# Splitting the query and key weights one unit ahead, and a split with the token tile as outer loop

## The chip, the cores and the metric

The kernel runs on one core of a Trainium2 chip. Its time is the device time of one execution in microseconds (us); a run's figure is the time of that core. The engines are TensorE (PE, with its weight loads listed as PEld), VectorE (DVE), ScalarE (ACT), GpSimd (POOL) and SyncE (SP, which here only starts transfers). Each works through its own queue in order.

## What is computed

One layer of a decoder for 256 tokens of width 2048, with 256 memory tokens, all in float32. After a norm, one wide projection feeds four branches; gates weigh them, and an output projection closes the layer. Cut to what matters here:

```python
h = rms_norm(x, g_pre[l])
proj = h @ w_in[l]
(a_val, a_gate, sq, sk, sv, s_gate, cq, ck, cv, c_gate, c_lr,
 mq, m_gate, g_logits) = jnp.split(proj, split_at, axis=-1)
...
y_c = gla_mixer(cq, ck, cv, c_lr, c_gate, w_alpha[l], b_alpha[l], g_gla[l])
y_m = mem_attn(mq, m_gate, mem, g_mem[l], w_mem_kv[l])
gates = jax.nn.sigmoid(g_logits.reshape(B, S, N_BRANCH, D_MODEL) + b_merge[l])
merged = (gates[:, :, 0] * (y_a @ w_br_pool[l]) + gates[:, :, 1] * (y_b @ w_br_swa[l])
          + gates[:, :, 2] * (y_c @ w_br_gla[l]) + gates[:, :, 3] * (y_m @ w_br_mem[l]))
x = x + rms_norm(merged @ w_out[l], g_post[l])
```

The change touches the projections `cq` and `ck` (queries and keys of the gated linear attention), the key and value projections of the memory tokens ahead of them, and every block that is computed by `a_block`, among them the output projection `merged @ w_out`.

## The kernel before

**Split numbers.** Every float32 operand of a large matmul is split into a high part in the reduced type fp32r and a low part, the remainder. `split_w` does this for a piece of 1024 weight columns: ACT copies the raw weights to the high part (a tile named ...h), DVE subtracts it from the raw weights (a tile named ...l). A product is then three matmuls, high by high, high by low and low by high. The parts live in rings of five tiles each (`NB_HILO`), so a split waits until PE has read the split five before it. The raw weights come by transfers of up to 1 MB, started by SP, into a ring of thirteen buffers that the activations and other large tiles share.

**Two forms of a block.** `b_unit` computes 128 output columns for all 256 tokens: it loads the weights, splits them in two halves (`cq0` has `cq00` and `cq01`), and runs 16 pairs of matmuls, one with the high part against both parts of the activations (512 wide) and one with the low part (256 wide). Then `evac` reads the accumulator out, for `cq` and `ck` by `two_sums`: one copy on ACT and one addition on DVE. `b_split` does the split alone, so that it can stand earlier in the program; before, that is done for the unit `cq0` only. `a_block` computes up to 512 output columns with the tokens on the partitions, in two accumulators (`t` = 0, 1), one for each 128 tokens. It goes through the weights split by split, in each split over the pieces `kk`, in each piece over `t`, with the three matmuls of `mm3` innermost. It returns a function that reads out both accumulators; the caller calls it at once.

**Background work.** `queue` holds generators: the memory keys' read-out (`km_evac`: four evacuations of `km_acc`, then a norm), and `quarter_prep`, which builds sums and differences of quarters of the activations (DVE subtracts to `qs`, ACT and DVE split that to `quarter`). `pull(n)` runs n steps of the first one, at fixed points of the blocks; `drain` runs one to its end. From the third `ck` unit on `gates` does the same for the gate projections, whose weights are named gu, gt and gv.

**What sets the order.** The program is written as one stream; a scheduler then gives each engine its own order and places the waits. `tc.issue_after(i)` makes what is traced inside it stand behind instruction `i` on the engine of `i`. Before, it is used for the memory keys' evacuation (behind the split of `cq0`) and for the scaling of the memory values (behind the latest split).

**The stages that the prediction speaks of.** First the memory tokens' values and keys (`vma`, `kma`) with the norm of x and its four pieces `xhl` (line 309 forms the normed piece, 225 and 226 split it), then `cq0` to `cq3` and `ck0` to `ck3` (lines 191 and 192 are the two matmuls of a pair, 139 and 140 the split, 203 to 207 the evacuation), then the blocks `cv` with the first gates between them, and so on; the output blocks `o0` to `o3` come near the end (145 to 147 are the matmuls of `mm3`, 947 and 948 read an output block out).

Of the kernel before, what the change touches and what calls it, by code (L numbers as in the profile page):

```python
# [14 lines left out]
P = 128  # L15
# [5 lines left out]
SCALE = DH ** -0.5  # L21
# [16 lines left out]
def kernel(ctx, tc, ins, out):  # L38
# [34 lines left out]
    queue = []  # L73

    def pull(n):
        while n > 0 and queue:
            try:
                next(queue[0][1])
                n -= 1
            except StopIteration:  # L80
                queue.pop(0)

# [41 lines left out]

    last_split = [None, None]

    def new_raw():
# [20 lines left out]

    def a_block(name, units, stat, nw, evac, load=None, per_split=None, other=False):

        accs = [seven(f"{name}a{t}") if other else acc(f"{name}a{t}", [P, 512]) for t in range(2)]
        nk = 4 * len(units)
        for u, src in enumerate(units):
            raw = load_raw(src, 4 * nw) if load is None else load(u, src)
            nk_s = max(1, 1024 // nw) if per_split is None else per_split(u)
            for hf in range(4 // nk_s):
                hi, lo = split_w(raw[:, hf * nk_s * nw : (hf + 1) * nk_s * nw], nk_s * nw, f"{name}{u}{hf}")
                for kk in range(nk_s):
                    k = 4 * u + nk_s * hf + kk
                    ws = slice(kk * nw, (kk + 1) * nw)  # L160
                    for t in range(2):
                        sh, sl = stat(k)
                        ts = slice(t * P, (t + 1) * P)
                        mm3(accs[t][:, :nw], sh[:, ts], sl[:, ts], hi[:, ws], lo[:, ws], k == 0, k == nk - 1)
                if hf % 2 == 0:
                    pull(1)
                gates(nk_s * 6 * (nw / 2.4 + 14) * 1e-3)
            pull(1)
# [11 lines left out]
    def b_unit(name, src, mov, evac, ready=None):  # L180
# [4 lines left out]
        for hf in range(2):  # L185
            hi, lo = ready[hf] if ready else split_w(raw[:, hf * 1024 : (hf + 1) * 1024], 1024, f"{name}{hf}")
            for kk in range(8):
                k = 8 * hf + kk
# [4 lines left out]
            if hf == 0:  # L193
                pull(1)
                gates(2.8)
        evac(name, a)
        pull(1)
# [79 lines left out]
    def m_norm():  # L277
        yield from inv_rms_row("m", mcol)
        yield
        km, vm = kv["k"], kv["v"]  # L280
        with tc.issue_after(last_split[0]):
            for t in range(2):
                act.activation(vm[:, t, :], vm[:, t, :], AF.Copy, scale=mcol[:, t : t + 1])
# [30 lines left out]
    vm_acc = [acc(f"vma{t}", [P, 512]) for t in range(2)]  # L314
    km_acc = [seven(f"kma{h}") for h in range(4)]

    def mem_chunk(c):
# [37 lines left out]
        for j in range(2):  # L355
            hi, lo = split_w(rk[:, 1024 * j : 1024 * j + 1024], 1024, f"km{c}{j}")
            for i in range(2):
                a = km_acc[2 * j + i]
# [11 lines left out]
    def km_evac():  # L370
        km = kv["k"] = c4("km", [P, 4, T])
        for h in range(4):
            with tc.issue_after(cq0_split[0]), tc.issue_after(cq0_split[1]):
                two_sums(f"km{h}", km_acc[h], km[:, h, :])
            yield
# [3 lines left out]
    drain("xprep")  # L379
    cq0 = b_split("cq0", ins["w_cqk"][0])  # L380
    cq0_split = tuple(last_split)

# [283 lines left out]

    for h in range(4):
        b_unit(f"cq{h}", ins["w_cqk"][h], h_at, plain_evac(gq[:, h, :], SCALE), cq0 if h == 0 else None)
    for h in range(4):
        if h == 2:  # L670
            drain("quarters")
            gate_stream[0] = all_gates()
        b_unit(f"ck{h}", ins["w_cqk"][4 + h], h_at, plain_evac(gk[:, h, :]))
    for j in range(3):
# [277 lines left out]
    def o_at(k):  # L952
        return mTh[k // 4][:, k % 4, :], mTl[k // 4][:, k % 4, :]

    for j in range(3):
        a_block(f"o{j}", [ins["w_out"][j, u] for u in range(4)], o_at, 512, o_evac(j, 512 * j, 512), other=j % 2 == 1)()
    a_block("o3", [ins["w_last"][0, u] for u in range(4)], o_at, 256, o_evac(3, 1536, 256), other=True)()
    for t in range(2):
# [109 lines left out]
```

## Time and profile before

| | before |
|---|---|
| median of the runs shown | 1192.18 us (1189.82 to 1192.59, 3 runs) |
| the profiled execution | 1190.69 us |
| its span, first to last instruction | 1188.5 us |
| mean granted clock of PE | 0.993 |
| DMA | 303.94 MB, mean 256 GB/s |

The span is the time between the first and the last instruction; the profiled execution takes 2.19 us more than that. Matmuls are pipelined, so a row's duration overlaps the next row, and the spacing of two starts says how long one costs. A wait in a view is put down to the engine that released it last. The granted clock is the share of full speed at which PE was allowed to run in a stretch.

### The profile page before, as it was taken

What the parts mean: (1) busy time and instruction counts of PE and PEld (TensorE: products, weight loads), DVE (VectorE), ACT (ScalarE), POOL (GpSimd) and SP (SyncE); (2) the same over time, 40 slices, a digit from 0 to 9 for tenths busy, and PEclk for the clock granted to TensorE, in tenths of its full rate; (3) what the DMA queues carried; (4) which work ended last, traced back from release to release, by engine and by line L of the source; (5) the groups of instructions that cost most, each with busy time, mean ns of one, the idle gap of its engine ahead of it and who ended that gap; (6) DMA issues with size and microseconds to landing.
All of it is one profiled execution on the core that took longest, in us unless ns stands there. A gap on an engine that the chain in (4) does not pass through costs nothing.

```text
span 1188.5 us, 15408 instructions
## 1 busy us (share of the span) xinstructions
PE 1157.8 (97%) x5854; PEld 974.5 (82%) x5854; DVE 960.9 (81%) x1201; ACT 646.2 (54%) x823; POOL 59.3 (5%) x109
## 2 busy tenths in 40 slices
PE   9888999999999999999999999999999999999997
PEld 7777888877888888878888887888888888888787
DVE  7966978999899789879988997997998676767454
ACT  7635546676655555565566565556655543444341
POOL 0100000000001001000000000000000102110000
PEclk9998999999999999999999999999999999999999
DMA  9644768776877588777788777776878988659321
GB/s 359 268 145 149 262 214 321 274 260 214 300 275 260 209 288 316 275 252 249 270 283 304 277 275 262 270 265 220 293 244 302 372 315 301 251 216 366 110 71 72
DMA packets 79946, 303.94 MB, mean 256 GB/s; under 512 B 6224, under 2 KB 8656, under 8 KB 57344
## 3 DMA queue, kind: packets, MB, share of 16 engines
q1 hardware_dynamic: 65568, 268.45, 62.8%
q0 software_dynamic: 8976, 24.91, 6.0%
q10 hardware_dynamic: 5328, 9.60, 2.2%
q8 instruction: 46, 0.75, 0.2%
q14 instruction: 28, 0.23, 0.0%
HBM read 285.11 MB, written 17.83 MB: 255 GB/s over the span
## 4 chain that ended last, share of the span: by engine, by line
PE 73%; DVE 6%; DMA 3%; ACT 2%; issue 2%; DVEq 0%; ACTq 0%; POOLq 0%; POOL 0%
PE q L145 5%; PE q L146 5%; PE q L147 5%; DMA raw<-in_w_g 2%; PE p L145 1%; PE p L146 1%; PE p L147 1%; DMA raw<-in_w_cg 1%; PE o1a L146 1%; PE sv2a L146 1%; PE sv0a L145 1%; DMA gd<-c 1%; PE sv0a L147 1%; PE sv0a L146 1%; PE sv2a L145 1%
## 5 line engine op out<-in xcount | busy, mean ns | idle before, releaser
L468 DVE TENSOR_TENSOR raw<-raw 128x1024 f32<-128x1024 f32 x64 | 77.9, 1218 | 10.2 <-DMA raw<-in_w_g 10.1
L474 DVE TENSOR_TENSOR raw<-raw 128x512 f32<-128x512 f32 x64 | 44.3, 694 | 1.1
L469 DVE TENSOR_TENSOR raw<-raw 128x512 f32<-128x512 f32 x64 | 44.3, 693 | 0.5
L892 POOL DMA_DIRECT2D g<-gd x32 | 17.5, 554 | 98.6 <-DVE merged L900 66.7
L900 DVE TENSOR_TENSOR merged<-merged,g 128x512 f32<-128x512 f32 x24 | 15.5, 684 | 0.0
L684 POOL DMA_DIRECT2D cgd<-cgate x4 | 2.2, 552 | 227.5 <-DVE cgate L220 227.5
L827 PE MATMUL sp<-k,q 128*128 128x128 f32 (+1 forms) x48 | 10.2, 335 | 1.3 <-DVE k L205 1.3
L859 POOL DMA_DIRECT2D ybd<-ybt x4 | 2.7, 678 | 173.7 <-DVE ybt L226 173.7
L948 DVE TENSOR_TENSOR yg<-o0a,gpost 128x512 f32<-128x512 f32 x2 | 1.4, 692 | 11.3 <-ACT oj L947 11.3
L827 PEld LDWEIGHTS sp<-k,q 128*128 128x128 f32 x48 | 7.4, 190 | 3.2 <-DVE k L205 1.8
L835 ACT ACTIVATE s<-s,st 128x384 f32<-128x384 f32 (+1 forms) x8 | 6.1, 768 | 5.7 <-DVE st L834 5.7
L830 DVE SCALAR_TENSOR_TENSOR s<-big_cst,sp 128x128 f32<-128x128 f32 (+1 forms) x24 | 7.1, 346 | 1.8 <-PE sp L827 1.7
L436 ACT ACTIVATE c<-c 128x512 f32<-128x512 f32 x8 | 5.0, 628 | 5.4 <-DVE c L482 3.8
L913 ACT ACTIVATE mTh<-mtp 128x512 fp32r<-128x512 f32 x8 | 4.3, 596 | 6.3 <-PE mtp L911 6.3
L225 ACT ACTIVATE xhl<-xn 128x1024 fp32r<-128x1024 f32 x4 | 4.2, 1058 | 6.4 <-DVE xn L309 6.4
L191 PE MATMUL ck0a<-xhl,ck00h 128*128 128x512 f32 x8 | 5.2, 649 | 2.5 <-ACT ck00h L139 2.5
L947 ACT ACTIVATE oj<-o0a 128x512 f32<-128x512 f32 x2 | 1.2, 597 | 11.9 <-PE o0a L147 11.9
L641 POOL TENSOR_TENSOR ms<-ms,half 128x2 f32<-128x2 f32 x4 | 5.7, 1430 | 35.1 <-DVE ms L640 35.1
L853 PE MATMUL po<-pt,sv 128*128 128x256 f32 x24 | 7.2, 384 | 0.2 <-ACT pt L848 0.2
L191 PE MATMUL ck1a<-xhl,ck10h 128*128 128x512 f32 x8 | 4.2, 533 | 3.2 <-ACT ck10h L139 3.2
L629 POOL TENSOR_TENSOR sq<-sq 128x256 f32<-128x256 f32 x4 | 4.6, 1156 | 52.6 <-ACT sq L628 45.0
L337 DVE SCALAR_TENSOR_TENSOR mhl<-mr,vecs,mhl 128x256 fp32r<-128x256 f32 x16 | 6.8, 479 | 0.5 <-issue 0.3
(4603 smaller groups left out, 4600.5 us busy)
## 6 DMA issues: line engine op xcount, KB each, us to landing
raw<-in_w_g SPq DMA_DIRECT2D x112, 1024.0 KB, 5.9
raw<-in_w_sqk SPq DMA_DIRECT2D x24, 1024.0 KB, 6.8
raw<-in_w_sv SPq DMA_DIRECT2D x12, 1024.0 KB, 6.2
raw<-in_w_out SPq DMA_DIRECT2D x12, 1024.0 KB, 9.1
raw<-in_w_cqk SPq DMA_DIRECT2D x8, 1024.0 KB, 11.3
raw<-in_w_cg SPq DMA_DIRECT2D x8, 1024.0 KB, 6.0
raw<-in_w_av SPq DMA_DIRECT2D x8, 1024.0 KB, 5.5
raw<-in_w_ag SPq DMA_DIRECT2D x8, 1024.0 KB, 5.8
```

The source lines that it names most:

```text
L145: ten.matmul(o, lhsT=sh, rhs=wh, start=start, stop=False, skip_group_check=again)
L146: ten.matmul(o, lhsT=sh, rhs=wl, start=False, stop=False, skip_group_check=again)
L147: ten.matmul(o, lhsT=sl, rhs=wh, start=False, stop=stop, skip_group_check=again)
L191: ten.matmul(a[:], lhsT=hi[:, ws], rhs=mov.both(k), start=(k == 0), stop=False)
L468: vec.tensor_tensor(r4[:, :, 0, :], r4[:, :, 0, :], r4[:, 1, :, :], op=ALU.add)
L469: vec.tensor_tensor(r4[:, 1, 1, :], r4[:, 1, 1, :], r4[:, 0, 0, :], op=ALU.add)
L474: vec.tensor_tensor(r4[:, 0, 1, :], r4[:, 0, 1, :], r4[:, 1, 1, :], op=ALU.add)
L827: ten.matmul(parts[g], lhsT=q3[:, g, it * P : (it + 1) * P], rhs=k3[:, g, :nj], start=True, stop=True)
L830: vec.scalar_tensor_tensor(s[:, g, :], dist[:, g, :], SLOPES[g * 4 + hh], parts[g], op0=ALU.mult, op1=ALU.add)
L853: ten.matmul(po[:], lhsT=sv[g][:, 0, vs], rhs=pt[g][:, 0:T], start=(g == 0), stop=False)
L892: pool.dma_start(gs[t][:], gate_dram[b, j, t][:])
L900: vec.tensor_tensor(m, m, gs[t][:], op=ALU.add)
```

## The change

It has three parts.

The loops of `a_block` are turned: in each split `t` is now outside `kk`, so that all matmuls of the split for the first 128 tokens come ahead of those for the second. `a_block` also takes `late`, the read-out of the block before, and traces it behind its own first split; the four output blocks hand it on in this way.

Each of the units `cq1` to `ck2` is split by `b_split` one unit ahead, before the unit in front of it is computed. `cq0` is split inside the last memory chunk, behind that chunk's last split.

From there until the gates begin, `pinned` is set: every step of the background queue, and the read-out of each unit, is traced inside `behind()`, which puts it behind the latest split on ACT and DVE.

```diff
+    last_split = [None, None]
+    pinned = [False]
+    def behind():
+        stack = ExitStack()
+        for i in last_split:
+            stack.enter_context(tc.issue_after(i))
+        return stack
+    def step(gen):
+        if not pinned[0]:
+            return next(gen, True)
+        with behind():
+            return next(gen, True)
     def pull(n):
         while n > 0 and queue:
-            try:
-                next(queue[0][1])
+            if step(queue[0][1]):
+                queue.pop(0)
+            else:
                 n -= 1
-            except StopIteration:
-                queue.pop(0)
...
-    def a_block(name, units, stat, nw, evac, load=None, per_split=None, other=False):
+    def a_block(name, units, stat, nw, evac, load=None, per_split=None, other=False, late=None):
...
-                for kk in range(nk_s):
-                    k = 4 * u + nk_s * hf + kk
-                    ws = slice(kk * nw, (kk + 1) * nw)
-                    for t in range(2):
+                if late is not None:
+                    with behind():
+                        late()
+                    late = None
+                for t in range(2):
+                    ts = slice(t * P, (t + 1) * P)
+                    for kk in range(nk_s):
+                        k = 4 * u + nk_s * hf + kk
+                        ws = slice(kk * nw, (kk + 1) * nw)
                         sh, sl = stat(k)
-                        ts = slice(t * P, (t + 1) * P)
                         mm3(accs[t][:, :nw], sh[:, ts], sl[:, ts], hi[:, ws], lo[:, ws], k == 0, k == nk - 1)
...
-        evac(name, a)
+        if pinned[0]:
+            with behind():
+                evac(name, a)
+        else:
+            evac(name, a)
...
             hi, lo = split_w(rk[:, 1024 * j : 1024 * j + 1024], 1024, f"km{c}{j}")
+            if c == 3 and j == 1:
+                ahead["cq0"] = b_split("cq0", ins["w_cqk"][0])
+                pinned[0] = True
...
-            with tc.issue_after(cq0_split[0]), tc.issue_after(cq0_split[1]):
-                two_sums(f"km{h}", km_acc[h], km[:, h, :])
+            two_sums(f"km{h}", km_acc[h], km[:, h, :])
...
-    for h in range(4):
-        b_unit(f"cq{h}", ins["w_cqk"][h], h_at, plain_evac(gq[:, h, :], SCALE), cq0 if h == 0 else None)
-    for h in range(4):
-        if h == 2:
+    cqk = [(f"c{'qk'[n // 4]}{n % 4}", ins["w_cqk"][n]) for n in range(8)]
+    for n in range(8):
+        if n == 6:
             drain("quarters")
+            pinned[0] = False
             gate_stream[0] = all_gates()
-        b_unit(f"ck{h}", ins["w_cqk"][4 + h], h_at, plain_evac(gk[:, h, :]))
+        if n < 6:
+            ahead[cqk[n + 1][0]] = b_split(*cqk[n + 1])
+        evac = plain_evac(gq[:, n, :], SCALE) if n < 4 else plain_evac(gk[:, n - 4, :])
+        b_unit(*cqk[n], h_at, evac, ahead.pop(cqk[n][0], None))
...
+    late = None
     for j in range(3):
-        a_block(f"o{j}", [ins["w_out"][j, u] for u in range(4)], o_at, 512, o_evac(j, 512 * j, 512), other=j % 2 == 1)()
-    a_block("o3", [ins["w_last"][0, u] for u in range(4)], o_at, 256, o_evac(3, 1536, 256), other=True)()
+        late = a_block(f"o{j}", [ins["w_out"][j, u] for u in range(4)], o_at, 512, o_evac(j, 512 * j, 512),
+                       other=j % 2 == 1, late=late)
+    a_block("o3", [ins["w_last"][0, u] for u in range(4)], o_at, 256, o_evac(3, 1536, 256), other=True, late=late)()
```

On SP and POOL the two kernels have the same rows in the same order. On the other engines the order differs in a few places. Rows name the line, the operation and what it writes and reads; a number behind a name is that of the buffer.

The first place is ACT's queue from the evacuation of `cq3` (`cq3s`) on, before:

```order
L203 ACTIVATE cq3s<-cq3a 128x256
L225 ACTIVATE quarter_552<-qs_755 128x512
L225 ACTIVATE quarter_553<-qs_756 128x512
L139 ACTIVATE ck00h<-raw_788 128x1024
L139 ACTIVATE ck01h<-raw_788 128x1024
L203 ACTIVATE ck0s<-ck0a 128x256
L225 ACTIVATE quarter_554<-qs_757 128x512
L225 ACTIVATE quarter_551<-qs_862 128x512
L139 ACTIVATE ck10h<-raw_840 128x1024
L139 ACTIVATE ck11h<-raw_840 128x1024
```

The same place of ACT's queue in the changed kernel, which has `ck00h` and `ck01h` further up, ahead of `cq2s`:

```order
L224 ACTIVATE cq3s<-cq3a 128x256
L246 ACTIVATE quarter_552<-qs_769 128x512
L152 ACTIVATE ck10h<-raw_797 128x1024
L152 ACTIVATE ck11h<-raw_797 128x1024
L224 ACTIVATE ck0s<-ck0a 128x256
L246 ACTIVATE quarter_553<-qs_770 128x512
L246 ACTIVATE quarter_554<-qs_771 128x512
L152 ACTIVATE ck20h<-raw_849 128x1024
L152 ACTIVATE ck21h<-raw_849 128x1024
L152 ACTIVATE gu0000h<-raw_931 128x1024
```

The split of a unit now stands behind the evacuation of the unit two before it (`ck10h` behind `cq3s`), where it stood behind that of the unit just before (`ck10h` behind `ck0s`); on DVE the low halves moved in the same way.

The second place is ACT's queue between the output blocks `o0` and `o1`, before (`oj` is the read-out of an accumulator of `o0`):

```order
L139 ACTIVATE o031h<-raw_9600 128x1024
L947 ACTIVATE oj_9634,ossq<-o0a_9496 128x512
L947 ACTIVATE oj_9637,ossq<-o0a_9497 128x512
L139 ACTIVATE o100h<-raw_9642 128x1024
L139 ACTIVATE o101h<-raw_9642 128x1024
L139 ACTIVATE o110h<-raw_9676 128x1024
```

and in the changed kernel:

```order
L152 ACTIVATE o031h<-raw_9600 128x1024
L152 ACTIVATE o100h<-raw_9636 128x1024
L152 ACTIVATE o101h<-raw_9636 128x1024
L973 ACTIVATE oj_9642,ossq<-o0a_9496 128x512
L973 ACTIVATE oj_9645,ossq<-o0a_9497 128x512
L152 ACTIVATE o110h<-raw_9676 128x1024
```

The two splits of the first weights of `o1` moved ahead of the two read-outs; between the later output blocks the order of before has that form already and stays.

The third place is PE's queue in the second split of `o1`, before (`o1a_9640` and `o1a_9641` are the accumulators of the two token tiles):

```order
L145 MATMUL o1a_9640<-o101h,mTh_8889 128x512
L146 MATMUL o1a_9640<-o101l,mTh_8889 128x512
L147 MATMUL o1a_9640<-o101h,mTl_8890 128x512
L145 MATMUL o1a_9641<-o101h,mTh_8889 128x512
L146 MATMUL o1a_9641<-o101l,mTh_8889 128x512
L147 MATMUL o1a_9641<-o101h,mTl_8890 128x512
L145 MATMUL o1a_9640<-o101h,mTh_8889 128x512
```

and in the changed kernel, where the two accumulators are `o1a_9634` and `o1a_9635`:

```order
L158 MATMUL o1a_9634<-o101h,mTh_8889 128x512
L159 MATMUL o1a_9634<-o101l,mTh_8889 128x512
L160 MATMUL o1a_9634<-o101h,mTl_8890 128x512
L158 MATMUL o1a_9634<-o101h,mTh_8889 128x512
L159 MATMUL o1a_9634<-o101l,mTh_8889 128x512
L160 MATMUL o1a_9634<-o101h,mTl_8890 128x512
L158 MATMUL o1a_9635<-o101h,mTh_8889 128x512
```

The second piece `kk` of the first token tile moved ahead of the first piece of the second tile; the matmuls are the same.

More of the change, by code (lines that the diff above doesn't have):

```diff
@@ L123 @@
     raw_count = [0]
-    last_split = [None, None]
     def new_raw():
@@ L280, in m_norm @@
         km, vm = kv["k"], kv["v"]
-        with tc.issue_after(last_split[0]):
+        with behind():
             for t in range(2):
@@ L315 @@
     km_acc = [seven(f"kma{h}") for h in range(4)]
+    ahead = {}
     def mem_chunk(c):
@@ L379 @@
     drain("xprep")
-    cq0 = b_split("cq0", ins["w_cqk"][0])
-    cq0_split = tuple(last_split)
     quarter = [e8(f"quarter{i}", [P, 2, 8, P], R) for i in range(4)]
```

## The prediction

> **What bounds the kernel now.** I read the page first: its span line and the row of engine totals.
>
> ```profile
> span 1188.5 us, 15408 instructions
> PE 1157.8 (97%) x5854; PEld 974.5 (82%) x5854; DVE 960.9 (81%) x1201; ACT 646.2 (54%) x823; POOL 59.3 (5%) x109
> ```
>
> TensorE (PE) is busy 97% of the span, so the kernel ends when PE has worked off its queue. A change that leaves the number of matmuls alone can only take out PE's idle time, 30.7 us, and time in which matmuls run slowly. So next I asked the view of waits for PE alone (columns: what waited, on whom, us in total, times, longest).
>
> ```profile
> PE ck1a L191 <- ACT ck10h L139: 3.2, 1, 3.2
> PE ck0a L191 <- ACT ck00h L139: 2.5, 1, 2.5
> ...
> PE o1a L145 <- ACT o100h L139: 1.7, 1, 1.7
> PE cq0a L192 <- DVE cq00l L140: 1.4, 1, 1.4
> ...
> PE ck1a L192 <- DVE ck10l L140: 0.8, 1, 0.8
> PE cq0a L191 <- ACT cq00h L139: 0.7, 1, 0.7
> ...
> PE ck0a L192 <- DVE ck00l L140: 0.5, 1, 0.5
> ```
>
> Six of these rows belong to three units of one stage, the query and key projections cq0, ck0 and ck1: 3.2 + 2.5 + 1.4 + 0.8 + 0.7 + 0.5 = **9.1 us**, each a wait for the high half (ScalarE, ACT) or the low half (VectorE, DVE) of a split weight. The fourth place is o1, the second output block. The windows view shows the same stage by its clock (columns: stretch, its length, busy us of PE, PEld, DVE, ACT, POOL, granted clock, DMA share, GB/s).
>
> ```profile
> 54.90:82.50 27.60, 25.57 (x139) 21.83 (x137) 16.12 (x24) 11.82 (x18) 4.27 (x6) 0.94 0.43 155
> 82.50:106.40 23.90, 16.94 (x67) 13.41 (x67) 13.36 (x16) 9.69 (x13) 0.00 (x0) 0.79 0.31 100
> 106.40:155.00 48.60, 48.60 (x258) 43.07 (x256) 40.82 (x46) 26.19 (x34) 0.00 (x0) 1.00 0.66 232
> ```
>
> The clock is down exactly where PE waits, 0.94 and 0.79, and 1.00 behind it, where PE has no idle time at all. A matmul of ck0 behind its wait is listed with 0.63 us, the same shape in cq2 with 0.40; and from cq2's first matmul to cq3's, a unit of 16 pairs at full rate takes 5.65 us, 0.353 a pair:
>
> ```profile
> 71.10 0.40 PE L191 MATMUL cq2a<-xhl,cq20h 128*128 128x512 f32 x1
> 76.75 0.40 PE L191 MATMUL cq3a<-xhl,cq30h 128*128 128x512 f32 x1
> 88.03 0.63 PE L191 MATMUL ck0a<-xhl,ck00h 128*128 128x512 f32 x1
> ```
>
> The lost clock is 27.6 x 0.06 + 23.9 x 0.21 = 1.7 + 5.0 = **6.7 us**. Together the stage loses about 15.8 us.
>
> **Why it waits, and what the new order does there.** In before, ACT reaches ck1's split only behind the evacuation of ck0 (which waits for ck0's last matmul) and behind two quarter copies:
>
> ```profile
> 95.19 0.38 ACT L203 ACTIVATE ck0s<-ck0a 128x256 f32<-128x256 f32 x1 [8.55 <-PE ck0a L192]
> ...
> 97.20 1.04 ACT L139 ACTIVATE ck10h<-raw 128x1024 fp32r<-128x1024 f32 x1
> ```
>
> Two microseconds lie between the two rows, and ACT had idled 8.55 us before the first: the split could have been done there. It is not the amount of work that delays it but its place in the queue. In the changed order ck0's split stands ahead of cq2's evacuation and ck1's ahead of ck0's. SP's and POOL's orders do not change, so no load is moved past another. What each split now has in hand:
>
> ```profile
> 50.82 1.06 ACT L225 ACTIVATE xhl<-xn 128x1024 fp32r<-128x1024 f32 x1
> 44.69 2.86 DVE L309 SCALAR_TENSOR_TENSOR xn<-xn,vecs,xrow 128x256 f32<-128x256 f32 x7
> 99.42 1.22 DVE L140 TENSOR_TENSOR ck11l<-raw,ck11h 128x1024 fp32r<-128x1024 f32 x1
> 100.55 1.22 DVE L140 TENSOR_TENSOR ck20l<-raw,ck20h 128x1024 fp32r<-128x1024 f32 x1
> 55.03 0.95 PE L253 MATMUL mpc<-ones,msq 128*128 128x2 f32 x8
> ```
>
> *cq0.* The third quarter of the activations is copied from 50.82 to 51.88; then DVE does its low half (1.14), cq0's two low halves (1.13 each, start to start in the two rows of 1.22), and the last four norm products (4 x 0.41); ACT copies the last quarter (1.06) and DVE does its low half (1.22): 51.9 + 1.14 + 2.26 + 1.64 + 1.06 + 1.22 = 59.2. PE is free at 55.03 + 0.95 = 55.98 and needs that quarter only at its thirteenth pair, 55.98 + 12 x 0.353 = 60.2. The price of splitting first, a later last quarter, is hidden by 1.0 us; without that cover it would cost its lateness one for one. cq0's wait of 2.1 us goes.
>
> *cq1 to ck1.* PE then runs units of 5.65: cq0 ends at 61.6, cq1 67.3, cq2 72.9, cq3 78.6, ck0 84.2, and, with the two bias matmuls of line 431 between them (2 x 0.23, the spacing shown further down), ck1 at 90.4. ck1's split is the first behind cq3's evacuation and one quarter copy, so its low half is ready near 78.6 + 0.4 + 0.6 + 1.05 + 1.2 = 81.9, 2.8 us ahead of use. ck2's stands behind ck0's evacuation and two copies, the second of which waits for a DVE subtraction: 84.2 + 0.45 + 1.0 + 0.65 + 1.05 + 1.2 = 88.6, still 1.8 us ahead. The waits added by the pinning (a copy queued behind a split that waits for its slot, such as ck01's until cq2's first half is read at 70.1) hold up ACT's cq2 evacuation, due only at 72.9; so they cost nothing. PE would reach ck2 at 90.4 instead of 106.44: 16.0 us earlier.
>
> ```profile
> 106.44 0.40 PE L191 MATMUL ck2a<-xhl,ck20h 128*128 128x512 f32 x1
> ```
>
> *What is late next: DVE.* From ck0's evacuation to ck30's low half the new order gives DVE ten splits, eleven half-size operations and three gk additions, one after the other:
>
> ```profile
> 107.06 0.42 DVE L205 TENSOR_TENSOR gk<-ck1a,ck1s 128x256 f32<-128x256 f32 x1 [3.02 <-ACT ck1s L203]
> 107.40 0.68 DVE L393 TENSOR_TENSOR qs<-xn,qs 128x512 f32<-128x512 f32 x1
> 108.00 0.69 DVE L393 TENSOR_TENSOR qs<-xn 128x512 f32<-128x512 f32 x1
> 119.32 1.22 DVE L140 TENSOR_TENSOR ck30l<-raw,ck30h 128x1024 fp32r<-128x1024 f32 x1
> 127.38 1.22 DVE L140 TENSOR_TENSOR ck31l<-raw,ck31h 128x1024 fp32r<-128x1024 f32 x1
> 129.01 0.28 PE L192 MATMUL ck3a<-xhl,ck31l 128*128 128x256 f32 x1
> ```
>
> Start to start they take 1.13, 0.60 and 0.34, so 11.3 + 6.6 + 1.0 = 18.9, and 0.5 of waiting for ck20's high half. From 84.2 + 0.45 that puts ck30's start at 104.1, where it stood at 119.32: **15.2 us earlier**, less than PE's 16.0. Before, ck31's low half was ready at 128.60 and used at 129.01, a slack of 0.41. So PE keeps 15.2 + 0.4 = **15.6 us**; its bounds are 15.2 (no slack) and 16.0 (DVE no limit). The loads follow, since SP waits for DVE's splits. Behind that DVE waits for PE again: it idles 6.12 us before cv100, whose high half stands on ACT behind the evacuation of cv0. So the gain is carried on.
>
> ```profile
> 156.43 0.88 DVE L140 TENSOR_TENSOR cv100l<-raw,cv100h 128x692 fp32r<-128x692 f32 x1 [6.12 <-ACT cv100h L139]
> ```
>
> **The output block.** ACT's o100h stood behind the two evacuations of o0, and those wait for PE:
>
> ```profile
> 1110.19 0.60 ACT L947 ACTIVATE oj<-o0a 128x512 f32<-128x512 f32 x1 [11.86 <-PE o0a L147]
> 1111.45 1.05 ACT L139 ACTIVATE o100h<-raw 128x1024 fp32r<-128x1024 f32 x1
> 1110.44 0.39 PE L147 MATMUL o0a<-o031h,mTl 128*128 128x512 f32 x1
> 1113.82 0.50 PE L146 MATMUL o1a<-o100l,mTh 128*128 128x512 f32 x1 [0.53 <-DVE o100l L140]
> ```
>
> ACT sat idle 11.86 us with the split to do. Now both halves of o1's first pair of splits stand ahead of the evacuations. The row at 1113.82 is o1's third matmul; at 0.23 a matmul it would stand at 1110.44 + 3 x 0.23 = 1111.13. **2.7 us** go. The evacuations move back by nothing, since ACT is through the splits long before o0 ends; o1's third split starts where o100h did, at 1111.45, so both its halves are there at 1111.45 + 1.05 + 1.2 = 1113.7, and PE needs them two splits into o1, at 1110.67 + 24 x 0.23 = 1116.2.
>
> **The loop turned.** t outside kk moves matmuls among themselves and adds none. I cost it at nothing: runs on one accumulator and a change of accumulator follow at the same 0.23.
>
> ```profile
> 109.51 0.39 PE L146 MATMUL p<-gu0000l,xhl 128*128 128x512 f32 x1
> 109.74 0.39 PE L147 MATMUL p<-gu0000h,xhl 128*128 128x512 f32 x1
> 1108.40 0.39 PE L147 MATMUL o0a<-o031h,mTl 128*128 128x512 f32 x1
> 1108.63 0.39 PE L145 MATMUL o0a<-o031h,mTh 128*128 128x512 f32 x1
> ```
>
> **Sum.** 15.6 + 2.7 = 18.3 us. The profiled execution took 1190.69 us, 2.19 more than its span; less 18.3 it is 1172.4. The median of the runs shown is 1192.18, 1.49 above the profiled one, so I expect **1173.9 us**. About 0.3% (3.6 us) is what a measurement of this kernel can tell from no change.
>
> **Rivals.** *(1) Only the waits go; the clock stays low.* For it: the halved rate outlasts the wait (the 0.63 row at 88.03 stands behind ck0's, not in it). Against: the same kind of unit ran cq2 and cq3 at full rate, and every drop follows a wait at once. It gives 18.3 - 6.7 = 11.6, so 1180.6. Chance 0.06. The Trainium skill, "TensorE: Matmul & The Clock Gate", section "HAM oscillation — how this bites in real kernels", bears on this: it asks for an idle gap above about 3.4 us. By that rule cq0's 2.1 and ck0's 3.0 would not have halved the clock and only ck1's share, an estimated half of the 5.0, would go, for about 1178; the trace disagrees, since the rate is halved right behind both shorter waits.
>
> *(2) A new wait in the stage,* at ck2 (1.8 us in hand) or at cq0's last quarter (1.0). If DVE comes over 2 us late there, the clock falls too: the smallest such event of before, cq0's, cost 2.1 + 1.7 = 3.8 us, those of ck0 and ck1, 7.0 + 5.0, 6.0 each. So 1177.7 to 1179.9. Chance 0.12.
>
> *(3) Given back downstream.* Between 155 and 275 us DVE is busy 109.18 of 120 and PE waits for it several times:
>
> ```profile
> 155.00:275.00 120.00, 116.67 (x599) 98.64 (x598) 109.18 (x129) 76.89 (x98) 1.67 (x3) 1.00 0.71 256
> ```
>
> If DVE and loads there kept a pace of their own, only o1's 2.7 would be left: 1189.5. Against: DVE enters that stretch behind PE (cv100), so its start moves too. Chance 0.05.
>
> *(4) Slower: matmuls on one accumulator.* The blocks cv, sv, o (10 of 96 matmuls) and the 24 units of the branches (24 each) make 1536 matmuls that now come in runs of six or more on one accumulator instead of three. If such a run cost time, 18.3 us / 1536 = 12 ns a matmul would cancel the gain, and 20 ns would give 1173.9 + 30.7 = 1204.6. The equal 0.23 spacings above speak against it. Chance 0.03.
>
> **Chances and range.** Forecast 0.74, the rivals 0.06, 0.12, 0.05 and 0.03. Faster by over 0.3%: 0.74 + 0.06 + 0.12 = 0.92; within it 0.05; slower 0.03. The bounds of the stage (15.2 to 16.0) and the spread of the runs shown, 2.8 us, give 1171.5 to 1176 around the forecast. For 8 in 10 I reach to 1180 for (2), and to 1170.5 below, should smaller waits close as well.
>
> **What would show it.** In the profile after: no wait of cq0, ck0, ck1 or o1 above 0.5 us; clock 1.00 from 55 us on; ck2's first matmul near 90.4; ck30's low half near 104; o1's first matmul 0.23 behind o0's last; spacing in the a-blocks still 0.23. Half-rate matmuls without a wait ahead would mean (1); a wait at ck20l or the last quarter (2); ck2 near 90 but cg at its old place (3); wider spacing (4).

## The result, and the profile after

| | before | after |
|---|---|---|
| median of the runs | 1192.31 us (1189.82 to 1192.59, 4 runs) | 1171.78 us (1170.65 to 1172.68, 4 runs) |
| ratio after / before | | 0.9832, 95% interval 0.9815 to 0.9849 |
| the profiled execution | 1190.69 us | 1172.68 us |
| its span | 1188.5 us | 1170.6 us |

The changed kernel is faster by 1.7%. The span is 17.9 us shorter; 18.3 had been forecast. First the page of the changed kernel, its span and the row of engine totals:

```profile
span 1170.6 us, 15411 instructions
...
PE 1149.8 (98%) x5854; PEld 968.2 (83%) x5854; DVE 961.2 (82%) x1201; ACT 647.0 (55%) x823; POOL 59.0 (5%) x109
```

PE's busy time fell by 8.0 us with the same 5854 matmuls; most of that is the clock, since four stretches of 3.413 us at half rate are gone (the last section), worth up to 6.8 us. Its idle time, span less busy, fell from 30.7 to 20.8 us. The view of waits for PE (what waited, on whom, us in total, times, longest) now begins so:

```profile
PE p L158 <- ACT p1c L480: 2.4, 4, 0.9
PE cv1a L158 <- ACT cv100h L152: 1.2, 1, 1.2
```

None of the rows of cq0, ck0, ck1 and o1 is left; the largest single wait of the kernel is now 1.2 us. The windows view of the changed kernel, with the same stretches as before the change (length, busy us of PE, PEld, DVE, ACT, POOL, granted clock, DMA share, GB/s):

```profile
54.90:82.50 27.60, 27.60 (x164) 24.23 (x163) 21.41 (x33) 14.95 (x22) 4.23 (x6) 1.00 0.43 155
82.50:106.40 23.90, 23.21 (x118) 18.95 (x117) 22.43 (x28) 15.80 (x21) 0.00 (x0) 1.00 0.59 198
106.40:155.00 48.60, 46.81 (x253) 41.19 (x252) 38.32 (x44) 23.43 (x30) 0.00 (x0) 1.00 0.63 219
```

The clock is 1.00 in all three. In the second stretch PE does 118 matmuls where it did 67. But PE has idle time again, 0.69 us in the second and 1.79 in the third, where it had none in the third before. The timeline of the changed kernel shows the places (start, us, engine, line, operation; the bracket is the idle time ahead and who ended it):

```profile
90.42 0.40 PE L208 MATMUL ck2a<-xhl,ck20h 128*128 128x512 f32 x1
...
102.41 0.50 PE L158 MATMUL p<-gu0020h,xhl 128*128 128x512 f32 x1 [0.69 <-ACT p1c L480]
...
114.45 0.38 PE L209 MATMUL ck3a<-xhl,ck31l 128*128 128x256 f32 x1
...
141.78 0.59 PE L158 MATMUL cv1a<-cv100h,xhl 128*128 128x346 f32 x2 [1.22 <-ACT cv100h L152]
```

Set beside the same matmuls of before, the first use of a split by PE moved like this:

| first matmul on | before | after | moved by |
|---|---|---|---|
| ck20h, ck2's first | 106.44 | 90.42 | -16.02 |
| gu0020h, behind the copy p1c | 117.53 | 102.41 | -15.12 |
| ck31l | 129.01 | 114.45 | -14.56 |
| cv100h | 156.45 | 141.78 | -14.67 |
| gt310bh, late in the gates | 848.64 | 833.53 | -15.11 |
| o101h, in the output block | 1116.22 | 1098.35 | -17.87 |

So 16.0 us were gained up to ck2, about 1.4 of it was lost again by cv1, and o1 added 2.76. What was lost between ck2 and ck31 has two causes, both in a place that the prediction had not looked at. The first is the row at 102.41. Before, ck2's second half stood on PE between the fourth and the fifth piece of the first gate (gu0011 and gu0020), and ACT copied the accumulator p to p1c behind it. Now that half has its split early and goes between gu0000 and gu0001, so nothing covers the copy: from gu0011's last matmul at 101.33 to gu0020's first at 102.41 are 1.08 us where 0.23 is the spacing. The second is ACT's queue further on, before (two rows) and after (two rows), and DVE's after:

```profile
122.57 1.06 ACT L139 ACTIVATE gt000ah<-raw 128x1024 fp32r<-128x1024 f32 x1 [3.62 <-DVE raw L469]
123.54 0.58 ACT L436 ACTIVATE c<-p 128x512 f32<-128x512 f32 x1
```

```profile
108.18 0.60 ACT L459 ACTIVATE c<-p 128x512 f32<-128x512 f32 x1 [4.60 <-PE p L160]
108.68 1.05 ACT L152 ACTIVATE gt000ah<-raw 128x1024 fp32r<-128x1024 f32 x1
```

```profile
104.14 1.22 DVE L153 TENSOR_TENSOR ck30l<-raw,ck30h 128x1024 fp32r<-128x1024 f32 x1
...
109.76 1.23 DVE L153 TENSOR_TENSOR gt000al<-raw,gt000ah 128x1024 fp32r<-128x1024 f32 x1 [1.81 <-ACT gt000ah L152]
```

Two rows changed places: the read-out of p, which waits for PE's last matmul on it, now stands ahead of the split gt000ah. ACT idles 4.60 us, DVE 1.81, and from ck30l to ck31l DVE takes 9.03 us (104.14 to 113.17) where it took 8.06 (119.32 to 127.38). It is the old mistake in a new place: a split behind an evacuation. The two causes hang together, since PE's last matmul on p, which the read-out waits for, comes later by what PE lost at gu0020.

The output block, on PE:

```profile
1095.41 0.39 PE L160 MATMUL o0a<-o031h,mTl 128*128 128x512 f32 x1
1095.63 0.39 PE L158 MATMUL o1a<-o100h,mTh 128*128 128x512 f32 x1
```

0.22 us lie between o0's last matmul and o1's first; nothing is lost there any more.

### The profile page after: what moved, and what is told of

Read it like the earlier page. It is cut to its first block, busy times and chain, and to the rows that moved or that the text cites. A ratio compares the mean times of both kernels' runs of the same rounds, so it can differ in the third digit from the quotient of the medians.

```text
span 1170.6 us, 15411 instructions
## 1 busy us (share of the span) xinstructions
PE 1149.8 (98%) x5854; PEld 968.2 (83%) x5854; DVE 961.2 (82%) x1201; ACT 647.0 (55%) x823; POOL 59.0 (5%) x109
## 4 chain that ended last, share of the span: by engine, by line
PE 76%; DVE 5%; DMA 3%; ACT 2%; issue 2%; DVEq 0%; POOLq 0%; POOL 0%; ACTq 0%
PE q L158 5%; PE q L159 5%; PE q L160 5%; DMA raw<-in_w_g 2%; PE p L158 2%; PE p L159 1%; PE p L160 1%; PE sv2a L159 1%; PE sv0a L158 1%; PE sv0a L160 1%; PE o0a L160 1%; PE sv2a L158 1%; PE o0a L158 1%; PE sv1a L158 1%; PE sv0a L159 1%
## 5 line engine op out<-in xcount | busy, mean ns | idle before, releaser
L459 ACT ACTIVATE c<-p 128x512 f32<-128x512 f32 x8 | 4.7, 587 | 5.1 <-PE p L160 5.1
L812 POOL DMA_DIRECT2D yad<-yat x4 | 2.7, 686 | 88.5 <-DVE yat L247 88.5
L359 ACT ACTIVATE mhl<-mr,vecs 128x256 fp32r<-128x256 f32 x16 | 6.9, 495 | 0.2 <-DMA mr<-in_memT 0.2
```

The costliest lines, as they stand in the source:

```text
L459: act.activation(dst, src, AF.Tanh, scale=0.5)
```

## The experiments

### Which part of the change carries the gain

**Late read-outs alone.** The kernel before, with only the output blocks' read-outs handed on (loop not turned, no split ahead):

```diff
+                if late is not None:
+                    with tc.issue_after(last_split[0]), tc.issue_after(last_split[1]):
+                        late()
+                    late = None
...
-        a_block(f"o{j}", [ins["w_out"][j, u] for u in range(4)], o_at, 512, o_evac(j, 512 * j, 512), other=j % 2 == 1)()
+        late = a_block(f"o{j}", [ins["w_out"][j, u] for u in range(4)], o_at, 512, o_evac(j, 512 * j, 512),
+                       other=j % 2 == 1, late=late)
```

> The kernel of before with one part of the change alone: the read-outs of the output blocks o0 to o2 are issued behind the first split of the next block; loops and query/key stage as before. My theory (a split stuck behind a read-out): o1's third matmul comes 0.7 us after o0's last instead of 3.4, so the span falls by 2.7 us, 0.23%, and nothing else moves; the waits and the half-rate matmuls at cq0, ck0 and ck1 stay (clock 0.94 and 0.79 there). Rival (the read-outs now come late and block the next step): a new wait at o110 or o2 gives the 2.7 us back, span within 0.5 us of before.

Measured: 1186.97 us, ratio 0.9963 (0.9948 to 0.9978), profiled span 1182.5. o1's waits are gone, and from sq211h, a unit late in the program (-3.1 us against before), to o101h (-6.0) 2.9 us are gained, which is the term of o1. But 3.1 us were there already, ahead of the edit: 2.0 by ck2's first matmul, of which about 1.7 come from the clock, which did not drop at cq0 in this execution although cq0 waited as before, and 1.1 in small differences further on. What decided at cq0 is worked out in the last section.

**The turned loop alone,** on the kernel before:

```diff
-                for kk in range(nk_s):
...
-                    for t in range(2):
+                for t in range(2):
+                    ts = slice(t * P, (t + 1) * P)
+                    for kk in range(nk_s):
```

> The kernel of before with the token tile as outer loop of a split in a_block, and nothing else. My theory: no effect, span within 0.7 us of before, spacing of the matmuls of o0 still 0.23 us on one accumulator and across a change. Rival (runs of six on one accumulator cost time): 1536 matmuls at 12 ns more would be 18 us slower, at 20 ns 31 us. Second rival (the turned loop carries part of the gain): some us faster, then the 18 us of the change are not all from the waits.

Measured: 1190.94 us, ratio 0.9994 (0.9983 to 1.0005), the same waits as before. Runs of six on one accumulator cost nothing; 1536 matmuls at 12 ns would have been 18.4 us, 1.5%.

**The splits ahead with the pinned order,** that is the changed kernel with the loop turned back and the output blocks read out at once:

```diff
-                for t in range(2):
...
-                    for kk in range(nk_s):
+                for kk in range(nk_s):
...
+                    for t in range(2):
...
-        late = a_block(f"o{j}", [ins["w_out"][j, u] for u in range(4)], o_at, 512, o_evac(j, 512 * j, 512),
-                       other=j % 2 == 1, late=late)
+        a_block(f"o{j}", [ins["w_out"][j, u] for u in range(4)], o_at, 512, o_evac(j, 512 * j, 512), other=j % 2 == 1)()
```

> The changed kernel without the turned loop and without the late read-outs of the output blocks: only the query/key splits one unit ahead with the pinned background steps. My theory: ck2's first matmul at 90.4 as in the changed kernel (106.4 before), clock 1.00 in the whole stage, cv1 at about 141.8, span 15 us below before; o1 still waits 1.7 + 0.5. Rival (only the 9.1 us of waits count, the clock is lost anyway): span 9 us below before.

Measured: 1176.22 us, ratio 0.987 (0.9855 to 0.9885). PE reaches ck1's second half 16.07 us earlier than before, o1's 1.7 + 0.5 us of waiting stay. The three parts alone gave 4.8, 0.8 and 15.6 us by their medians, 21.2 together; the whole change gave 20.5. So they add up within the spread of the runs of before; of the 4.8, the rows above give 2.9 to the edit.

**The splits ahead without the pinned order.** The changed kernel, without the one line that makes read-outs and background steps stand behind the splits:

```diff
                 ahead["cq0"] = b_split("cq0", ins["w_cqk"][0])
-                pinned[0] = True
```

> The changed kernel with the query/key splits written one unit ahead, but nothing pinned behind them; turned loop and late read-outs of the output blocks stay. In ACT's order cq00 then stands behind the last quarter of the activations again and ck10 behind ck0's evacuation; ck0's split stays ahead of cq2's evacuation. My theory (the place in the queue decides): cq0 waits about 2 us and runs 3.4 us at half rate, ck1 waits about 2.5 us and runs 3.4 or 6.8 us at half rate, ck0 waits no more. Left of the stage's loss: 3.8 + 4.2 to 6; span 8 to 11 us below before, and 7 to 10 above the changed kernel. Rival (writing the split ahead is enough and the pinning does nothing): as fast as the changed kernel, 18 us below before.

Measured: 1177.73 us (1175.75 to 1179.74), ratio 0.989 (0.987 to 0.9909). Four waits are back; in the view of waits:

```profile
PE cq0a L209 <- DVE cq00l L153: 1.4, 1, 1.4
...
PE ck1a L208 <- ACT ck10h L152: 0.8, 1, 0.8
PE ck1a L209 <- DVE ck10l L153: 0.8, 1, 0.8
PE cq0a L208 <- ACT cq00h L152: 0.7, 1, 0.7
```

PE is 12.1 us earlier than before at ck1, not 16.0. The pinning is worth 3.9 us there, 3.1 between the two spans (1173.7 and 1170.6), and about 6 between the medians, which come from different series of runs. I had expected more waiting, and the clock to fall with it. ck0 did not wait and ck1 only 1.6 us, and in the profiled execution the clock did not fall at all. But that execution is the fastest of the four. The two slowest, 1178.89 and 1179.74 us, have mean clocks of 0.996 and 0.994 where it has 0.998, so there it probably did fall, and the pinning is worth more than 3.1 us. Written earlier in the program, a split is not yet earlier on its engine; but most of the gain comes with that alone.

### What one wait costs

**ck1's split put back** to the start of its unit in the changed kernel, and, in the next kernel, **ck0's** (there `n != 3`):

```diff
-        if n < 6:
+        if n < 6 and n != 4:
```

> The changed kernel with ck1's split alone put back where its unit begins (ck0, ck2 and the rest stay ahead, so on ACT ck1's high half now stands behind ck2's two). It prices one wait of the kernel before. Worked out from the changed kernel's rows: PE is through ck0 and the bias matmuls at 84.2, ck10h is done near 88.65 and ck10l near 90.2: a wait of 4.4 + 0.8 = 5.2 us. Theory of the prediction (the clock is halved behind such a wait and comes back with it: the stage loses wait and clock): a half-rate stretch of 6.8 us behind it, 3.4 us more, less 1.5 us that the changed kernel loses to p1c and DVE further on and this one would not: 1178.5 to 1179.5 us. Rival 1 (the waits alone cost): no half-rate stretch, 1175.2 to 1176. Rival 3 (DVE and loads keep their own pace downstream and take the loss up): under 1174.

> The changed kernel with ck0's split alone put back where its unit begins, so on ACT ck00h stands behind ck1's two high halves. From the changed kernel's rows: PE is free at 78.5, ck00h is done near 81.9, ck00l near 83.5: a wait of 3.4 + 0.8 = 4.2 us. With the clock halved for 3.4 or 6.8 us behind it (1.7 or 3.4 us) and up to 0.6 us of DVE's limit taken up behind: 1177.1 to 1179.4 us. Without a drop of the clock: 1175.4 to 1176. Loss taken up downstream: under 1174.

Measured: 1178.49 us (1176.8 to 1179.87) with ck1's split in place and 1178.49 (1176.95 to 1178.65) with ck0's; ratios to the kernel before 0.9889 (0.987 to 0.9908) and 0.9889 (0.9871 to 0.9907). Each is 6.7 us above the changed kernel's 1171.78. The waits and the windows with ck1's split in place:

```profile
PE ck1a L208 <- ACT ck10h L152: 3.2, 1, 3.2
...
PE ck1a L209 <- DVE ck10l L153: 0.4, 1, 0.4
```

```profile
83.05:86.47 3.42, 1.27 (x6) 0.59 (x4) 1.94 (x3) 2.70 (x5) 0.00 (x0) 1.00 0.00 0
86.47:89.88 3.41, 1.91 (x4) 1.19 (x5) 3.41 (x5) 2.08 (x4) 0.00 (x0) 0.50 0.27 38
89.88:93.30 3.42, 3.42 (x12) 2.84 (x12) 2.74 (x3) 1.48 (x2) 0.00 (x0) 0.50 0.96 362
```

and the waits with ck0's in place:

```profile
PE ck0a L208 <- ACT ck00h L152: 3.2, 1, 3.2
...
PE ck0a L209 <- DVE ck00l L153: 0.9, 1, 0.9
```

With ck1's in place PE waited 3.65 us where I had reckoned 5.2, because one quarter copy now stood behind the splits on ACT and ck10h was done at 87.5, not 88.65. In both, 6.8 us at half rate follow, 3.4 us more. Behind ck1's second half PE is 6.1 us later than in the changed kernel, behind ck0's 7.3. Neither wait alone nor a loss that vanishes downstream fits: the price of one such wait is itself plus the clock, and most of it reaches the end: with ck0's in place 5.7 of the 7.3 us are left at o101h. With ck1's in place the loss shrinks from 6.1 us to 4.3 at cv0's second split (cv001h); ck2's second half stands between gu0011 and gu0020 again there, and the 1.5 us that the changed kernel gives back between ck2 and that place (-16.02 to -14.50) is not given back. (Its profiled execution lost the clock twice more further on, at cv1 and at 728 us, which is part of why its span, 1177.8, is 7.2 longer.)

### What was given back between ck2 and cv1

**The changed kernel once more,** as a mark for the kernels on the same chip:

> The changed kernel once more, as the mark for the three that share its chip: 1170.7 to 1172.7 us and ratio 0.982 to 0.985, as in its first runs. If the gain of 18.3 us hung on one chip or on when a clock drop falls, it would come out more than 3 us off. In its profile the wait of 0.69 for p1c at 102.4 us and the one of 1.22 for cv100h at 141.8 should stand again; whether the second one lowers the clock may differ.

Measured: 1172.43 us (1172.29 to 1174.31), ratio 0.9851 (0.9825 to 0.9876), the same waits at p1c (0.69) and cv1 (1.22 + 0.33).

**Only the first half of ck2 split ahead,** so that the second stands where it did and covers the copy p1c:

```diff
-    def b_split(name, src):
+    def b_split(name, src, halves=2):
...
-            ahead[cqk[n + 1][0]] = b_split(*cqk[n + 1])
+            ahead[cqk[n + 1][0]] = b_split(*cqk[n + 1], 1 if n == 5 else 2)
```

> Only the first half of ck2 is split ahead; the second is split where before had it. Theory (the new order lost 0.96 us at gu0020 because ck2's second half no longer stands between gu0011 and gu0020 on PE, so that the copy p1c is waited for): the wait of 0.69 for p1c at 102.4 us goes, ck2's second half stands between gu0011 and gu0020 again, PE is 0.7 to 1.0 us earlier than the changed kernel at 105 us, and the time is 1170.5 to 1171.2. Rival (DVE is the limit there anyway, as the sum of the prediction had it): the wait goes but the time comes back as waits for low halves at gt000 or ck31 between 108 and 116, shift at cv0 under 0.3 us, time as the changed kernel, 1171.8.

Measured: 1173.84 us (1173.14 to 1173.97), ratio 0.9858 (0.9833 to 0.9882): 1.4 us slower by the medians than the changed kernel beside it, whose range it lies within. The wait for p1c at gu0020 is gone, as the theory had it, but neither theory saw what came instead. ACT's queue and PE in this kernel:

```profile
90.36 0.39 ACT L230 ACTIVATE ck1s<-ck1a 128x256 f32<-128x256 f32 x1 [3.45 <-PE ck1a L215]
90.64 0.62 ACT L252 ACTIVATE quarter<-qs 128x512 fp32r<-128x512 f32 x1
91.16 1.05 ACT L152 ACTIVATE gu0000h<-raw 128x1024 fp32r<-128x1024 f32 x1
```

```profile
95.40 0.50 PE L159 MATMUL p<-gu0000l,xhl 128*128 128x512 f32 x1 [2.07 <-DVE gu0000l L153]
```

With one split fewer ahead, the first gate's split gu0000 fell behind the evacuation of ck1; in the changed kernel it starts at 88.09, ahead of it. So PE waited 2.07 us for its low half, and the clock dropped for 3.4 us. The edit removes the copy's wait and makes a larger one, so the time cannot price the copy's. The rows behind the new wait can: from the first matmul on gu0010h to that on ck31l this kernel takes 16.87 us (99.69 to 116.56), before took 17.01 (112.00 to 129.01) with one short matmul more. ACT has gt000ah ahead of the read-out of p again (110.00 and 110.97). So with ck2's half back in its place neither of the two losses is left.

### A version that is faster than both

cv1's wait, the largest left that one order makes, has the cause of o1's: cv100h stands on ACT behind the two read-outs of cv0. **The read-outs of the cv blocks handed on** like those of the output blocks:

```diff
+    late = None
     for j in range(3):
         c0, n = CV_BLOCKS[j]
-        a_block(f"cv{j}", [ins[f"w_cv{j}"][u] for u in range(4)], h_at, n, cv_evac(j))()
+        late = a_block(f"cv{j}", [ins[f"w_cv{j}"][u] for u in range(4)], h_at, n, cv_evac(j), late=late)
+    late()
```

> The read-outs of cv0 and cv1 are handed on behind the first split of the next block, as the change does it for o0 to o3. Theory (order on ACT alone makes cv1's wait, as it did o1's): the wait of 1.22 + 0.3 us at cv1 (141.8) goes, everything behind it is 1.2 to 1.5 us earlier, time 1170.2 to 1170.6; where the wait lowered the clock in an execution, 1.7 more. Rival (DVE, not ACT, sets when cv1 can start: its low half comes too late even if the high half is early): a wait on DVE cv100l takes its place, gain under 0.4 us. Third case: with two accumulator buffers for cv, cv1's second accumulator is cv0's second one and must wait for its late read-out; then the wait moves to the first matmul of cv1's second accumulator (or cv2's), and the time is 1171 to 1174.

Measured: 1168.31 us (1167.87 to 1172.62), ratio 0.9826 (0.9798 to 0.9854), against 1172.43 for the changed kernel on the same chip. ACT's queue in this kernel, and then three matmuls of it and of the changed kernel:

```profile
134.35 0.77 ACT L152 ACTIVATE cv100h<-raw 128x692 fp32r<-128x692 f32 x1
135.95 0.79 ACT L152 ACTIVATE cv101h<-raw 128x692 fp32r<-128x692 f32 x1 [0.83 <-PE cv0a L160]
139.59 0.46 ACT L550 ACTIVATE cv<-cv0a 128x348 f32<-128x348 f32 x1 [2.86 <-PE cv0a L160]
```

```profile
137.08 0.40 PE L158 MATMUL q<-gt003bh,quarter 128*128 128x512 f32 x1
...
177.97 0.47 PE L158 MATMUL q<-gv0020h,quarter 128*128 128x512 f32 x1
```

```profile
137.14 0.40 PE L158 MATMUL q<-gt003bh,quarter 128*128 128x512 f32 x1
...
181.21 0.47 PE L158 MATMUL q<-gv0020h,quarter 128*128 128x512 f32 x1 [0.17 <-DVE q L509]
```

Both splits are through 2.8 us before the read-outs start. The wait went, as the theory had it, but the gain is larger than its 1.2 to 1.5 us. From gt003bh to gv0020h 3.2 us are gained, twice the wait removed (1.55). A row's duration reaches into the next, so an idle time in a view is shorter than what the wait costs: counted by the starts, with 0.16 and 0.23 us as the spacings, the stop at cv1 cost 2.1 us and one at gt004 0.8. PE has no idle time in this stretch now.

**Once more, on another chip,** with **the loop turned back** beside it (`kk` outside `t`, as in the kernel before), since cv has only two accumulator buffers and its late read-out frees them late:

> The kernel with cv's read-outs handed on, once more, as the mark for the unturned one and to see whether its gain holds on another chip: 1168 to 1170 us, 2.5 to 4.5 under the changed kernel's 1171.8. If the 4.1 us on the first chip were 1.4 us of a wait removed and the rest chance, it would come out at 1170.4 or above.

> The same with the token tile as the inner loop again (kk outside t), so that both accumulators of a block are begun and ended side by side. Theory (the turn of the loop matters only where a block's second accumulator is still to be read when the block begins, that is with late read-outs and two accumulator buffers, as cv has them): the second accumulator of cv1 is wanted 0.5 us after the first instead of after half a split's matmuls, before cv0's late read-out has left it, so a wait of 1 to 3 us comes back at cv1 or cv2, and in the o blocks, which have buffers of their own, nothing changes: 1169.5 to 1172. Rival (the turn is without effect everywhere, as it was by itself at 0.9994): the same time as the turned kernel within 0.5 us.

Measured: 1168.61 us (1167.79 to 1169.57), ratio 0.981 (0.9789 to 0.983), so the gain holds: all these runs lie below all eight of the changed kernel (from 1170.65), while on the first chip the two ranges still touched (1172.62 and 1172.29); and 1168.45 (1167.84 to 1168.95), ratio 0.9808 (0.9788 to 0.9827), for the unturned one. My theory of the turn gave 1 to 3 us and fell. The wait that it named is there, but small; PE in the unturned kernel:

```profile
140.16 0.32 PE L160 MATMUL cv0a<-cv031h,xhl 128*128 128x348 f32 x1
140.55 0.43 PE L158 MATMUL cv1a<-cv100h,xhl 128*128 128x346 f32 x1
```

0.39 us apart, where 0.16 is the spacing and the turned kernel has 0.15 (140.22 to 140.37). A read-out of cv takes ACT 0.46 us, so there is little to hide. In the time the turn shows nowhere.

**Both edits,** cv's read-outs handed on and ck2 split half ahead:

> Both edits of the two kernels before. If they are independent, as the theory of separate waits has it, their gains add: 0.8 + 1.3 = 2.1 us under the changed kernel, 1169.3 to 1170.0. Rival (one takes up the slack of the other, DVE being nearly full from 100 to 145 us): no better than the better one of the two.

Measured: 1170.5 us (1169.58 to 1173.5), ratio 0.9835 (0.9808 to 0.9862): 2.2 above the kernel with cv's read-outs alone. The new wait at gu0000l stands here too, 2.1 us long and with half rate behind it. That outweighs what the edit was to gain, as it did without cv's late read-outs; by the medians it lost 1.4 us there and 2.2 here, which the spread of four runs each does not tell apart.

## Why the prediction was right, step by step

**The waits and the clock at cq0, ck0 and ck1.** Right. PE reached ck2 at 90.42; 90.4 was forecast. The clock came back with the waits, as the two kernels with one split put back show from the other side.

**cq0's last quarter.** Forecast: ready at 59.2 and used at 60.2. DVE's row of the last quarter's low half, and PE's of the thirteenth pair:

```profile
58.40 1.23 DVE L247 TENSOR_TENSOR xhl<-xn,xhl 128x1024 fp32r<-128x1024 f32 x1 [1.13 <-ACT xhl L246]
```

```profile
60.35 0.39 PE L208 MATMUL cq0a<-xhl,cq01h 128*128 128x512 f32 x1
```

Ready at 59.63 and used at 60.35: 0.7 us in hand, not 1.0, and enough. ck2's first low half was done at 87.27 + 1.23 = 88.50 (88.6 forecast), with 1.9 us in hand.

**DVE late next, PE keeps 15.6.** This step was 1.0 us too high. ck30's low half started at 104.14, forecast 104.1, so the sum over DVE's queue up to there was right. PE did not wait there (it used ck30 at 107.98, 2.6 us after that row's end); the step meant DVE to set the pace at ck31, and it did: ck31's low half was ready at 113.17 + 1.22 = 114.39 and used at 114.45, so the 0.4 us of slack was spent. What failed is that the step took DVE's way from ck30l to ck31l as unchanged. It grew by 0.97 us, because ACT's read-out of p had changed places with gt000ah, and because PE had lost 0.9 us to p1c before. At ck31l 14.56 were left, and 14.67 at cv1. The step followed DVE's queue alone from ck2 on; what was exchanged stands on ACT's.

**o1.** 2.7 forecast, 2.76 measured (-15.11 at gt310bh to -17.87 at o101h).

**The turn at nothing.** Right, 0.9994 (0.9983 to 1.0005).

**The sum and the offset.** 18.3 forecast, 17.9 by the spans: the step above lost 1.0, and 0.4 came back in small waits between 155 and 850 us that the prediction did not name. That its sum is off by only 0.4 us is in part luck. The profiled execution took 1172.68, forecast 1172.4. The last term failed: I added 1.49 us because the median of before lay that much above its profiled execution, and the median after, 1171.78, lies 0.9 below its own. Such an offset only says where one execution lay among the runs of its kernel; it does not carry over to another kernel. In all runs of these experiments the kernel before lay between 1187.28 and 1195.88 (42 runs), the changed one between 1170.65 and 1174.31 (8 runs); the clock drops, which differ from one execution to the next and of which the changed kernel shows none between its start and its last 6 us in its two profiles, are the likely reason for the wider spread. Only profiled executions show their clock in time, but the mean clock of 38 of the 42 is on record: it goes from 0.994 in the fastest (1187.28) to 0.987 in the slowest (1195.88), with a correlation of -0.71.

**The rivals.** (1), only the waits go, is refuted by the clock of 1.00 and by the two priced waits. The version of it by the idle gap of 3.4 us of the Trainium skill, "TensorE: Matmul & The Clock Gate", section "HAM oscillation — how this bites in real kernels", gave about 1178 and is refuted by the 1171.78. Where only the first half of ck2 is split ahead, a wait of 2.07 us was enough for half rate. (2), a new wait in the stage, did come, but at p1c on PE (0.69 us) and at gt000 on DVE (1.81), not at the two places named, and too short on PE to lower the clock. (3), given back downstream, is refuted: the -14.67 at cv1 has become -15.11 at gt310bh. (4) is refuted by the turned loop alone.

## What to carry to other kernels

When an engine in front has idle time and a consumer waits for it, look at its queue for a read-out or copy that itself waits for the consumer; what stands behind that read-out should stand ahead of it. Moving a piece of work forward also takes it away from where it was, so ask what it covered there, and compare the orders of every engine that feeds the bottleneck, past the point that you were looking at. A wait of PE of two to four microseconds is to be priced with the clock that may fall behind it, and a spread between executions of one kernel is a hint that it has such waits.

## What the runs showed of the clock

The same wait lowered the clock in some executions and not in others: cq0's 2.0 us did in the kernel before and not in the one with late read-outs alone, o1's 2.25 us not in before but with the turned loop, cv1's 1.55 us in two of the ten kernels that have that wait. In the trace's record of the granted clock all changes of one execution lie a multiple of 3.413 us apart (in before at 58.26, 61.67, 85.57, 92.40, 99.22 and 102.64 us), and this grid lies differently in each execution. A slot is here the stretch between two lines of the grid. The windows view, laid on the grid, for cq0 in the kernel before:

```profile
54.85:58.26 3.41, 1.62 (x11) 1.18 (x10) 2.25 (x3) 3.41 (x5) 1.64 (x1) 1.00 0.00 0
58.26:61.67 3.41, 3.17 (x10) 2.79 (x11) 3.41 (x5) 2.38 (x3) 1.40 (x3) 0.50 0.33 50
```

and in the kernel with the late read-outs alone:

```profile
52.98:56.39 3.41, 2.89 (x20) 2.52 (x19) 1.94 (x6) 1.91 (x3) 0.23 (x1) 1.00 0.00 0
56.39:59.80 3.41, 1.91 (x9) 1.46 (x10) 3.41 (x5) 3.41 (x6) 1.40 (x1) 1.00 0.00 0
```

In the first, 1.79 of the wait's 2.0 us fall into one slot, and the next slot runs at half rate. In the second the wait is cut by a slot's border into 0.52 and 1.50 us, and nothing happens. For o1 it is the same with the turned loop alone (2.20 us in one slot, then half rate) against before (1.72 and 0.53):

```profile
1109.56:1112.97 3.41, 1.21 (x5) 0.36 (x3) 2.49 (x4) 2.89 (x5) 0.00 (x0) 1.00 0.00 0
1112.97:1116.38 3.41, 3.35 (x8) 2.68 (x9) 3.41 (x5) 2.53 (x3) 0.00 (x0) 0.50 0.29 70
```

I summed PE's idle time by slot in the 14 profiles of this case, without the start-up and the last 15 us. Of the slots at full rate, all 13 with 1.78 us or more of idle time were followed by half rate, none with less than 1.49, and 4 of the 13 between (1.49 to 1.73). So about half a slot of idle time decides in these profiles, and a slot at half rate costs up to 1.7 us. In a slot already at half rate less sufficed to stay there: of six such slots with 0.47 us or more of idle time (up to 1.50), five were followed by a second one, which makes the drops of 6.8 us. By these counts a wait that leaves less than about 1.5 us of idle time in each slot is safe, one of more than 3.6 us has over 1.78 us in one slot wherever the border falls, and between them the place of the border decides. The Trainium skill, "TensorE: Matmul & The Clock Gate", section "What's actually happening", has the free-running window of 3413 ns, and the trace agrees: all changes lie on a grid of 3.413 us. Its rule against idle gaps above about 3.4 us, in the section "HAM oscillation — how this bites in real kernels", is too lax here: 1.79 us in one slot were enough.
